# Narrow matmuls widened to 128 rows, a filter layer cast in three pieces, and a new table of issue, in a one-core transformer step

## The chip, the cores and the metric

The kernel runs on one NeuronCore of a Trainium2 chip. A core has a matrix engine (TensorE, PE in the rows below, with its weight loads shown apart as PEld), a vector engine (DVE), a scalar engine (ACT), a pool engine (POOL) and a queue that issues most of the transfers (SP). The metric is the time of one execution in microseconds on the device, the median of several executions.

## The reference

One inference step of a trunk with two layers runs over 128 prompt tokens and 1024 latent tokens, with 1024 channels in float32. Layer 0 mixes with a Hyena long convolution beside a latent attention (MLA); layer 1 with a Conformer convolution beside a grouped-query attention (GQA); each layer ends in an MLP of 4096 units. What the change touches is this (shapes cut, names as in the reference):

```python
# Hyena filters: 33 features -> 64 -> 64 hidden units -> 4 x 512 channels, for n_tok positions
hid = jnp.sin(freq * (z @ w1 + b1))
hid = jnp.sin(freq * (hid @ w2 + b2))
h = (hid @ w3) * jnp.exp(-t[:, None] * jnp.abs(decay))
spec = jnp.fft.rfft(two_sided(h), axis=0)
# long convolution, twice
z = gate * (irfft(rfft(z, 2 * n) * spec) + skip * z)
# MLP of every layer
f = jnp.square(jax.nn.relu(h @ w1 + b1)) @ w2 + b2
# grouped-query attention (prompt tokens attend to prompt tokens)
s = einsum('bqhgd,bkhd->bhgqk', q, k) * scale
```

## The kernel before

Every product with full precision is made from rounded parts: a matrix is held as a high part and a low part of a 32-bit format that TensorE takes in one pass, and `mm3` (L584) issues high x high, high x low and low x high into one PSUM bank. The helper lines are what the rows name: `mm` is L582, the transposes by the identity `tr` L590, `tt` (two tensors on DVE or POOL) L593, `ts` L597, `act` L603, `cpy` (copies and casts on ACT) L606, and `ld` (loads and stores on the SP queue) L562. All tiles lie in one arena, `b` in the rows, whose places come from a table.

The work is staged so: the Hyena filters are made (`filter_hidden`, then `ht` for eight tiles of 128 positions in two orders, then `spectra`), the input projections follow, then the long convolutions (`hyena`), MLA, the output projection, the MLP of layer 0 in three chunks of 384 tokens, and the same for layer 1. Beside the filters and the convolutions, matmuls with `ada_w` run (`ada_steps`, 32 output columns, not rounded).

Some matmuls contract over fewer than 128 rows of the array. In `filter_hidden` the features have 33 rows and the hidden units 64. In `ht` (L847) the 128-row part `hid` holds the high part in rows 0 to 63 and the low part in rows 64 to 127, and a second matmul with 64 rows adds high x low of `w3` (36 of them). In `hyena.first` (L1088) one extra matmul per 128 frequencies has 3 rows (`zrow` with `s3`, 16). In `mlp` (L1755) the bias `b2` enters through `ones` with 33 rows, of which rows 0 and 32 are filled (36). In GQA the prompt's second product has 64 rows (8).

The order in which each engine's instructions are issued is not that of the code. `in_order` (L2480) reads ORDER, a packed table with one step for each instruction of PE, DVE, ACT, POOL and SP, and ties every instruction to the one that the table puts ahead of it. Waits between engines follow from the data and from the reuse of places in the arena.

## Time and profile before

| | |
|---|---|
| three executions | 3310.30, 3310.32, 3315.06 us (median 3310.32) |
| the profiled execution | 3319.34 us |
| its span, first to last instruction | 3317.6 us |
| mean granted clock of TensorE | 0.983 of full |
| instructions | 40,881 |

The rows below come from the profiled execution. A row of instructions gives their start, busy time, engine, line, operation and operands (for a matmul rows\*columns of the weights, then rows x moving columns), their count, and in square brackets how long the engine was idle ahead of them and what ended that. PE's ends are modelled, so times from start to start are safer than busy times.

### The profile page before, as it was taken

To read this page: it belongs to the slowest core of one execution; us is meant where nothing else is said; L and a number is where in the kernel's file an instruction comes from. 1 tells how busy PE (TensorE), PEld (TensorE's weight loads), DVE (VectorE), ACT (ScalarE), POOL (GpSimd) and SP (SyncE) were. 2 spreads that over 40 slices of the span, in tenths; PEclk is the share of its full clock that TensorE was granted. 3 is DMA by queue.
4 is the path that set the end of the run, shared out by engine and by line. 5 is a ranking of instruction groups with operands and counts; after the bars stand their busy time and mean duration, and the time that the engine had idled before them with its cause. 6 is when DMAs were issued, how large, how long until landed. Compare 5 with 4: busy or idle time off the path is not lost. (4 is left out here: it accounts for less than half of the span.)

```text
span 3317.6 us, 40881 instructions
## 1 busy us (share of the span) xinstructions
PE 3185.1 (96%) x15636; PEld 2567.1 (77%) x15636; DVE 2106.3 (63%) x3088; ACT 1242.7 (37%) x2024; POOL 826.2 (25%) x713
## 2 busy tenths in 40 slices
...
PEclk9999888999999999999999998999999999999999
...
GB/s 224 185 42 148 254 142 132 96 19 43 106 118 219 150 143 210 170 155 174 100 156 156 125 167 119 46 48 46 126 116 188 156 133 162 139 100 181 137 127 102
DMA packets 161028, 444.58 MB, mean 134 GB/s; under 512 B 17384, under 2 KB 63144, under 8 KB 159296
## 3 DMA queue, kind: packets, MB, share of 16 engines
...
HBM read 386.10 MB, written 54.73 MB: 133 GB/s over the span
## 5 line engine op out<-in xcount | busy, mean ns | idle before, releaser
L582 PE MATMUL P<-b,b 128*128 128x384 f32 (+9 forms) x14314 | 2989.5, 375 | 91.3 <-ACT b L606 28.8
L582 PEld LDWEIGHTS P<-b,b 128*128 128x128 f32 (+3 forms) x14314 | 2443.3, 188 | 595.0 <-issue 150.1
L593 DVE TENSOR_TENSOR b<-b,b 128x1024 fp32r<-128x1024 f32 (+12 forms) x1087 | 952.6, 902 | 620.2 <-ACT b L606 383.0
L606 ACT CAST b<-b 128x1024 fp32r<-128x1024 f32 (+3 forms) x595 | 538.8, 918 | 1099.4 <-DMA b<-w 498.6
L593 POOL TENSOR_TENSOR b<-b,b 128x1024 f32<-128x1024 f32 (+10 forms) x440 | 670.2, 1540 | 924.6 <-ACT b L603 443.8
L603 ACT ACTIVATE b<-P 128x512 f32<-128x512 f32 (+4 forms) x400 | 221.6, 573 | 244.5 <-PE P L582 214.0
L597 POOL TENSOR_SCALAR small<-small 128x1 f32<-128x1 f32 (+2 forms) x72 | 41.8, 581 | 1049.8 <-DVE small L1682 1021.0
L593 DVE TENSOR_TENSOR b<-P,b 128x512 f32<-128x512 f32 (+11 forms) x364 | 214.3, 611 | 135.8 <-PE P L582 73.6
L1454 DVE TENSOR_REDUCE small<-P 128x1 f32<-128x512 f32 (+1 forms) x384 | 216.0, 591 | 45.1 <-PE P L582 41.6
L593 DVE TENSOR_TENSOR b<-b 128x384 f32<-128x384 f32 (+1 forms) x200 | 116.8, 597 | 199.0 <-ACT b L603 195.7
L600 DVE SCALAR_TENSOR_TENSOR b<-b,dwhalf,b 128x376 f32<-128x376 f32 (+2 forms) x268 | 204.2, 804 | 1.1
L603 ACT ACTIVATE b<-P,b 128x384 f32<-128x384 f32 x192 | 108.9, 577 | 220.0 <-PE P L582 212.5
L606 ACT COPY b<-P 128x512 f32<-128x512 f32 (+3 forms) x165 | 71.3, 449 | 199.9 <-PE P L582 157.6
L590 PE MATMUL P<-ident,b 128*128 128x128 f32 (+3 forms) x774 | 127.2, 287 | 18.2 <-DVE b L593 10.1
L590 PEld LDWEIGHTS P<-ident,b 128*128 128x128 f32 (+3 forms) x774 | 96.2, 146 | 55.7 <-DVE b L593 18.2
L603 ACT ACTIVATE b<-b 128x384 fp32r<-128x384 f32 (+2 forms) x200 | 102.3, 528 | 34.7 <-DVE b L593 16.6
L582 PE MATMUL P<-b,sT 128*32 128x512 f32 x384 | 100.0, 630 | 12.3 <-DMA b<-ada_w 12.2
L600 DVE SCALAR_TENSOR_TENSOR b<-b,small,b 128x1024 f32<-128x1024 f32 x72 | 93.0, 1295 | 7.0 <-POOL small L593 6.7
L606 ACT CAST b<-P 128x512 fp32r<-128x512 f32 (+9 forms) x134 | 64.3, 507 | 72.0 <-PE P L590 58.8
L603 ACT ACTIVATE b<-P,modT 128x384 fp32r<-128x384 f32 (+2 forms) x104 | 58.5, 596 | 75.6 <-PE P L582 37.6
L597 DVE TENSOR_SCALAR b<-P,modT 128x384 f32<-128x384 f32 (+2 forms) x104 | 58.5, 580 | 32.4 <-ACT b L603 25.6
L603 ACT ACTIVATE b<-b,dwhalf 128x429 f32<-128x429 f32 (+2 forms) x92 | 55.9, 626 | 56.8 <-PE P L582 27.7
...
## 6 DMA issues: line engine op xcount, KB each, us to landing
b<-w SPq DMA_DIRECT2D x384, 512.0 KB
...
```

The costliest lines, as they stand in the source:

```text
L582: self.nc.tensor.matmul(out, lhsT, rhs, start=start, stop=stop)
L590: self.nc.tensor.transpose(out, in_, self.ident)
L593: (eng or self.nc.vector).tensor_tensor(out=out, in0=a, in1=b, op=op)
L597: (eng or self.nc.vector).tensor_scalar(out=out, in0=a, scalar1=s1, scalar2=s2, op0=op0, **kw)
L600: self.nc.vector.scalar_tensor_tensor(out=out, in0=a, scalar=s, in1=b, op0=op0, op1=op1)
L603: self.nc.scalar.activation(out=out, in_=in_, func=func, **kw)
L606: self.nc.scalar.copy(out=out, in_=in_)
L1454: nc.vector.tensor_reduce(out=m3[i][:, 4 * jj + pi : 4 * jj + pi + 1], in_=b(w), axis=AX.X, op=ALU.max)
```

## The change

1. The 64-row matmul of `ht` gets 128 rows: `columns` now makes the low part of `w3` in all 128 rows.
2. The 3-row matmul of `hyena.first` gets 128 rows; `zrow` and each of the four `s3` tiles are set to zero on POOL first.
3. The 33-row bias matmul of `mlp` gets 128 rows, with zeros in the others.
4. The 64-row product of the GQA prompt gets 128 rows; `gqa_keys` makes the low part of the prompt's keys in all rows with one more DVE operation for each of two key heads.
5. `filter_hidden` casts and subtracts its last layer in three pieces of 384 columns instead of one of 1152.
6. The tables of issue are new for all five engines. The table of places is the same (its checksum alone changes, since it counts calls).

```diff
@@ filter_hidden
-        self.cpy(hid.r(n), dst.f(n))
-        self.tt(hid.r(n)[64:128], dst.f(n)[64:128], hid.r(n)[64:128], ALU.subtract)
+        for o in (0, 384, 768):
+            h, v = hid.r(384, o), dst.f(384, o)
+            self.cpy(h, v)
+            self.tt(h[64:128], v[64:128], h[64:128], ALU.subtract)
@@ filter_spectra, columns
-            self.tt(w3.r()[0:64], w3f.f()[0:64], w3h.r()[0:64], ALU.subtract)
+            self.tt(w3.r(), w3f.f(), w3h.r(), ALU.subtract)
@@ filter_spectra, ht
                 self.mm(b(), hs, w3h.r(512, cols), True, False)
-                self.mm(b(), hs[0:64], w3.r(512, cols)[0:64], False, True)
+                self.mm(b(), hs, w3.r(512, cols), False, True)
@@ hyena
         zrow = self.ra(512)
+        g.memset(zrow.f(512), 0.0)
...
             s3 = self.ra(256)
+            g.memset(s3.f(256), 0.0)
@@ hyena, first
-                            self.mm(out, zrow.r(128, 128 * q)[0:3], s3.r(256)[0:3], False, True)
+                            self.mm(out, zrow.r(128, 128 * q), s3.r(256), False, True)
@@ mlp
-        nc.vector.memset(b2.f()[0:33], 0.0)
+        nc.vector.memset(b2.f(), 0.0)
...
-        self.cpy(b2h[0:33], b2.f()[0:33])
+        self.cpy(b2h, b2.f())
...
-                            self.mm(banks[jj][s](), ones[0:33], b2h[0:33, 512 * s : 512 * s + 512], True, False)
+                            self.mm(banks[jj][s](), ones, b2h[:, 512 * s : 512 * s + 512], True, False)
@@ gqa_keys
-                self.tt(k2.r(n, o)[0:64], b(n)[0:64], k1.r(n, o)[0:64], ALU.subtract)
+                w = min(n, KEYS - o)
+                self.tt(k2.r(w, o)[0:64], b(w)[0:64], k1.r(w, o)[0:64], ALU.subtract)
+                if w < n:
+                    self.tt(k2.r(n - w, o + w), b(n - w, o=w), k1.r(n - w, o + w), ALU.subtract)
@@ gqa
-            return dict(m=full, row=lambda o, n: h.r(n, o), s=(full, h65), x=(full, h64), bufs=(a, h))
+            return dict(m=full, row=lambda o, n: h.r(n, o), s=(full, h65), x=(full, full), bufs=(a, h))
...
-            k64 = lambda o, n: k2.r(n, o)[0:64]
-            return dict(m=full, s=(full, k65), x=(full, k64))
+            low = lambda o, n: k2.r(n, o)
+            return dict(m=full, s=(full, k65), x=(full, low))
@@ the table of issue
-ORDER_OF = 1470002208
+ORDER_OF = 3602219959
```

The table is packed, so its effect is shown by what stands in three places. In these rows each line is an instruction with its output and inputs; buffer numbers are counted in the order of the code, and run four to nine higher in the new program.

**Place 1, the start, on ACT.** b_147 is the filters' last hidden layer, b_171 its rounded form, b_117 the decay rows, negt the positions. Before:

```order
L603 ACTIVATE b_121<-b_121 64x384 x3
L603 ACTIVATE b_147<-b_147 128x384 x3
L606 CAST b_171<-b_147 128x1152
L603 ACTIVATE b_147<-b_117 128x1024
L603 ACT_TABLE_LOAD
L603 ACTIVATE b_208<-b_147,negt 128x512
```

And now:

```order
L603 ACTIVATE b_121<-b_121 64x384 x3
L603 ACTIVATE b_147<-b_147 128x384
L606 CAST b_171<-b_147 128x384
L603 ACTIVATE b_147<-b_147 128x384
L606 CAST b_171<-b_147 128x384
L603 ACTIVATE b_147<-b_147 128x384
L606 CAST b_171<-b_147 128x384
L603 ACTIVATE b_147<-b_117 128x1024
L603 ACT_TABLE_LOAD
L603 ACTIVATE b_212<-b_147,negt 128x512
```

Each piece of the cast now follows its sine, so two of the three are done when the last sine is.

**Place 2, the MLP of layer 0, on PE.** The row with ones_r is a bias matmul; the other rows are matmuls of the running layers. Before:

```order
L582 MATMUL P<-b_10210,b_12280 128x384
L582 MATMUL P<-b_10277,b_12278 128x384 x2
L582 MATMUL P<-b_9191,ones_r 128x512
L582 MATMUL P<-b_12575,b_11811 128x512
L582 MATMUL P<-b_12577,b_11811 128x512
L582 MATMUL P<-b_12575,b_11811 128x512
L582 MATMUL P<-b_10277,b_12280 128x384
```

And now:

```order
L582 MATMUL P<-b_10286,b_12482 128x384
L582 MATMUL P<-b_10357,b_12480 128x384
L582 MATMUL P<-b_9200,ones_r 128x512
L582 MATMUL P<-b_12584,b_11820 128x512
L582 MATMUL P<-b_12586,b_11820 128x512
L582 MATMUL P<-b_12584,b_11820 128x512
L582 MATMUL P<-b_10357,b_12480 128x384
```

A bias matmul still stands alone between wide ones; what surrounds it is a later pair of columns (b_10357 for b_10277).

**Place 3, the last long convolution, on PE and SP.** b_4713 and b_4726 (and b_5267 before, b_5276 now) are transposed by ident; b_5267 and b_5276 hold the cached latents, loaded from c_ckv into the place that one of the transposed tiles of the convolution leaves. PE before:

```order
L582 MATMUL P<-b_3111,b_4597 128x256 x2
L582 MATMUL P<-b_3111,b_4599 128x256
L582 MATMUL P<-b_3113,b_4653 128x256 x2
L582 MATMUL P<-b_3113,b_4654 128x256
L582 MATMUL P<-b_3115,b_4668 128x256 x2
L582 MATMUL P<-b_3115,b_4669 128x256
L590 MATMUL P<-ident,b_5267 128x128 x2
L582 MATMUL P<-b_3109,b_4502 128x256 x2
```

PE now:

```order
L590 MATMUL P<-ident,b_4729 3x128
L582 MATMUL P<-b_4852,b_4754 128x512
L582 MATMUL P<-b_4851,b_4754 128x512
L590 MATMUL P<-ident,b_4713 128x128
L590 MATMUL P<-ident,b_4726 128x128
L590 MATMUL P<-ident,b_4713 128x128
L590 MATMUL P<-ident,b_4726 128x128
L590 MATMUL P<-ident,b_5276 128x128 x2
L582 MATMUL P<-b_4786,b_3104 128x256
```

And SP, before:

```order
L562 DMA b_5064<-spec_181 128x4x256
L562 DMA b_5141<-spec_181 128x4x256
L562 DMA b_5267<-c_ckv 128x256
L562 DMA b_5270<-c_kr 128x64
L562 DMA b_5228<-xd 128x1024
```

SP now:

```order
L562 DMA b_5073<-spec_185 128x4x256
L562 DMA b_5150<-spec_185 128x4x256
L562 DMA b_5237<-xd 128x1024
L562 DMA b_5276<-c_ckv 128x256
L562 DMA b_5279<-c_kr 128x64
```

The two transposes of the cached latents moved about 70 rows up on PE, right behind the last transposes of the convolution's input, while their load moved one place down on SP. The load waits for the last transpose of b_4713 in the new program, as it did for that of the same tile before, because it takes that tile's place.

## Rows read from the trace of the kernel before

**Rows 1.** The page of the profile: the span, the busy time of the engines, and the 40 slices of PE and of its granted clock:

```profile
span 3317.6 us, 40881 instructions
...
PE 3185.1 (96%) x15636; PEld 2567.1 (77%) x15636; DVE 2106.3 (63%) x3088; ACT 1242.7 (37%) x2024; POOL 826.2 (25%) x713
...
PEclk9999888999999999999999998999999999999999
```

**Rows 2.** The same by stages (start:end, length, busy time of each engine with the instructions that began, mean granted clock of TensorE, DMA share, GB/s). The first is the making of the filter tiles; the second row the long convolutions; the third goes through MLA and the MLP of layer 0 into the second mixer; the fourth the second half of the Conformer mixer and the start of GQA; the fifth the rest, with the MLP of layer 1; the last row is a part of the first:

```profile
0.00:120.00 120.00, 106.28 (x314) 52.69 (x315) 85.17 (x127) 59.62 (x94) 54.23 (x50) 1.00 0.51 187
...
340.00:605.00 265.00, 204.39 (x1194) 155.08 (x1193) 211.39 (x362) 63.08 (x128) 143.07 (x113) 0.88 0.54 177
605.00:2000.00 1395.00, 1381.60 (x6828) 1118.87 (x6827) 868.34 (x1279) 544.68 (x862) 306.78 (x263) 1.00 0.39 135
2000.00:2260.00 260.00, 234.17 (x1067) 155.86 (x1065) 235.31 (x363) 127.37 (x236) 178.20 (x138) 0.94 0.19 68
2260.00:3317.00 1057.00, 1041.90 (x5070) 877.04 (x5069) 602.24 (x826) 387.81 (x586) 113.56 (x79) 1.00 0.38 133
...
44.70:120.00 75.30, 75.30 (x270) 40.77 (x270) 62.64 (x85) 35.27 (x58) 39.52 (x28) 1.00 0.32 115
```

**Rows 3.** Who waited for whom, PE alone, in the stretch 340 to 605 us (engine, line, releaser: us in total, times, longest):

```profile
PE P L582 <- ACT b L606: 23.0, 11, 6.4
PE P L582 <- DMA b<-ada_w: 12.2, 4, 6.4
PE P L590 <- DVE b L593: 9.6, 4, 4.4
```

**Rows 4.** Matmul groups of the whole span, shapes kept apart (xcount | busy us, mean ns | idle before):

```profile
L582 PE MATMUL P<-b,b 64*128 64x512 f32 x36 | 21.9, 619 | 0.0
...
L582 PE MATMUL P<-b,ones_r 33*128 33x512 f32 x36 | 17.3, 490 | 1.1 <-ACT b L603 1.1
...
L582 PE MATMUL P<-b,b 3*128 3x256 f32 x16 | 6.1, 381 | 0.0
...
L582 PE MATMUL P<-b,b 64*128 64x128 f32 x8 | 2.6, 325 | 0.0
```

**Rows 5.** The timeline of PE: a run of wide matmuls, a run with four 64-row ones in it (its name is that of its first), and the row that follows each:

```profile
64.91 6.92 PE L582 MATMUL P<-b,b 128*128 128x512 f32 x29
71.76 2.76 PE L582 MATMUL P<-b,sT 128*32 128x512 f32 x10
74.45 4.65 PE L582 MATMUL P<-b,b 64*128 64x512 f32 x13
79.03 1.48 PE L582 MATMUL P<-b,sT 128*32 128x512 f32 x6
```

**Rows 6.** The timeline of the weight loads at the start of the second of these runs (64\*128 is the narrow one):

```profile
74.45 0.18 PEld L582 LDWEIGHTS P<-b,b 64*128 64x128 f32 x1 [0.84 <-issue]
74.88 0.19 PEld L582 LDWEIGHTS P<-b,b 128*128 128x128 f32 x1 [0.24 <-issue]
75.31 0.18 PEld L582 LDWEIGHTS P<-b,b 64*128 64x128 f32 x1 [0.25 <-issue]
```

**Rows 7.** The timeline of PE around two bias matmuls of the MLP of layer 0, with the run between them:

```profile
1392.76 0.49 PE L582 MATMUL P<-b,ones_r 33*128 33x512 f32 x1
1393.18 2.34 PE L582 MATMUL P<-b,b 128*128 128x512 f32 x9
1395.45 0.49 PE L582 MATMUL P<-b,ones_r 33*128 33x512 f32 x1
```

**Rows 8.** The timeline of ACT at the start: the cast of all 1152 columns behind the last sine, and the first ten exponentials:

```profile
19.76 1.15 ACT L606 CAST b<-b 128x1152 fp32r<-128x1152 f32 x1
...
24.70 6.23 ACT L603 ACTIVATE b<-b,negt 128x512 f32<-128x512 f32 x10
```

**Rows 9.** The timeline of DVE there: the subtraction for `hid`, and one of the multiplications of PSUM with an exponential:

```profile
20.94 1.35 DVE L593 TENSOR_TENSOR b<-b,b 64x1152 fp32r<-64x1152 f32 x1 [1.77 <-ACT b L606]
...
35.74 0.69 DVE L593 TENSOR_TENSOR b<-P,b 128x512 f32<-128x512 f32 x1 [2.17 <-PE P L582]
```

**Rows 10.** The timeline of PE there, the first row with all of 33 matmuls, and the row that follows:

```profile
22.35 22.46 PE L582 MATMUL P<-b,b 128*128 128x512 f32 x33 [4.89 <-DVE b L593]
44.74 3.16 PE L582 MATMUL P<-b,sT 128*32 128x512 f32 x8
```

**Rows 11.** The narrow matmuls among the 33 of that stretch, 22.3 to 44.7 us:

```profile
L582 PE MATMUL P<-b,b 64*128 64x512 f32 x16 | 12.0, 772 | 0.0
```

**Rows 12.** Busy time of PE's matmuls in two stretches that hold one shape alone, 128x256 (length, PE and PEld busy with their counts, granted clock, DMA share, GB/s):

```profile
2031.40:2037.30 5.90, 5.88 (x27) 5.88 (x28) 0.50 0.25 94
536.20:543.80 7.60, 7.60 (x63) 7.29 (x61) 1.00 0.63 194
```

**Rows 13.** The timeline of PE at place 3 of the change: two three-row transposes, and further on those of the cached latents:

```profile
525.20 0.38 PE L590 MATMUL P<-ident,b 128*3 128x128 f32 x2
...
543.80 0.38 PE L590 MATMUL P<-ident,b 128*128 128x128 f32 x2
```

**Rows 14.** The timeline of SP there: the issue of the loads:

```profile
524.18 0.57 SPq L562 DMA_DIRECT2D b<-c_ckv  x1
...
527.49 0.33 SPq L562 DMA_DIRECT2D b<-xd  x1
```

**Rows 15.** A load of 256 KB whose landing the profile gives (KB each, median us from issue to landing):

```profile
b<-pdft POOLq DMA_DIRECT2D x3, 256.0 KB, 3.3
```

More of the change, by code (lines that the diff above doesn't have):

```diff
@@ L64 @@
 HY_ENG = 0, 1, 0, 1
-PLACES_OF = 968071531
+PLACES_OF = 3472302832
 PLACES = """
@@ new lines @@
++iAL{*53#PXepfgz?+Zm?wHK2E1sxrj3j;m>aHcmF<eh|{nPbo~oT2~6aM<{cb0PA7nj;7CWj&h7XuX@`Jm<|0<O_1wYhP8y2oC=+o94MdXT2x8;qjQ
+~IKLBy=pQl(3y?BZ|B^wRvC31<!B`e^z9-K^Ia@Ui3p3C&?h?M&rl!J02bYszV)7VQ##d<W-
+0ejY)Lqt0q$ez5LR$kbHZPn1@$eOHW*R|QP3sTpVUiTdB6+Vd_xsMpW)mNu8aK){I23QMXFT79Q58lY9<hV`4W>Ujk>eK|-
++PJ>j;b<2x9{f5_A}0Fc=m6Xv`or2W=vg<z#})ZJX!l*m{a1Xu0~31QjQ0Lmwq_&t$pO_>mUNb!C67~>Rpy6)eY$QowXaNvzDMWjT6m<crLsQbjINEK
+S~9<7HiB-
+g=>mDBpKIqCS1HLg;Y;D#0kHYEkjaiVNA4vlZr0U*E413{`mFrF4Bt}Rs?=gdS3@eB<rFsW@pR4JqTH@OKUi_Z84>x9QNl&={CTG>YnjdG+uB>PUvnF
@@ new lines @@
+9xlP8bfyJLu6dVc#C|m1b-5G1>!<1;?_df0W{ZZf$w8TqaMK+zS7uzPP&!uN{afr<^t--*5|V1-
+$M6I4mjPwZ6_t<w<MyfFFD&d>)`zmhuiI0dfk`5ONdJnd9L1r1?f`mi2C@UAN(kp(V`v<QBKT@U>sQ;&x5W!=td+k7HD$WuU6Gg&dGHlXTcdi*4_1+X
+I0|1159xj+DEokJFAv|G-
+U{4OORLq?V+LuMfmO2FhpbdD3T649c~XJ?Mp}zyCU?pB&M$Q+ry4X5<>DwB)l!`N@x>bVokR_T+t)T6g%m3+K$?JkvMWhvY9dI=nka*0ALkPU_=PM;9
+T#F|DX9{jnOTI~)Er`w&aAlOHtFi~g}^-<#jDlR|deT2p-
+QPdPavy8Y1akzbSd%5Pv!yi@Tm#e!^wet4_AwZpR)ag`WW_4g)b#d>&+yejh!yhg5+H|YOuhP_f=3Cr+*RJ=;j?`nf!-
+lAs#F9kjuNd3czuRq!WkI=Pi9O4OG{QuGN$#5pz-
@@ new lines @@
+M2)By;TmQl#ymmP)7QM`xU+fDJy@D&RFC{*$IPU?uOUhMtMz-gp=WElA|Oq>J$I_tiJvX!>M5FCeI|wql^2+51Wp8Dm+TMF-
+rf$SZKq?Lw}@p^<lKB%j9F>Qu&+Ei}U5LLyp7pupaCk0iAm1EeWD7_0@1hcE&%3Gh<dp$3KNZNcB^b>POYPA2bqvRB=rh4QKTkmxswuCKzP-c-
+jzn`p|h<5g!}^zppSVV?MYvuc?#cJYWZ_&DY&$)`>xWq)v?XJQMN<nU!QP-WPVliII@bH_JUXKV3g9ekY7FM-L=Ep(WQ#7G1liA9YHPPjy%-
+X<K*#<et=qXtS8o)gbyb2>az+mqp@zI{jk1Ga64>fpXxD-
+e;5zW+e5Iac!TS#nh%6cW!;Pb5dP?&ZBBJ`&fnzotDquD|0?D9;VxNx+EtuKU8jyoz%X+u0!+fw#^#HC*NN7=-gB?XMXam3~uuSvc5E~PO3|-
+B=w;2%3lwBkG5-
+S7O5U|O_%N0dhqYv!r5yXE~va5$HF4scI^Orc9Vdj#XN^S`<dzZJ+R*N%B}|_$EOmm*x%1G81nD(RU8W6iw^tU<{u7=yTU8vg^FQikwH4nAVf>lBL~=
@@ new lines @@
+(h_Nu{MG9mPm{o;TZ(rIvoLljHT1MdqdVe70{|V&;!opz^0?mI`TPw69sjaNZZOwi5Gf%9-
+Sp=Frr$9DrhGZQ67SXp#6W#7&ze+In^~)AzTLk=Q9=RgvYzC<S^k*7UoUdBV2Z3Y^hCThqDGfX{SNEUUyKqT;=o|JH`o7uQWgpUkcreZzJ=i;IofQ_+
+gJ=`r3>4!2%lu2KHvRb(`+dwsALqBUZVwLPb<n#JG87&1E=rP+pOfmHP>Q7&z0d)7SX&-
+&@GN?aBl9YRWd;`7wCH}_=g)~XXQU#ga6gXQ$aum<Xz&oz5(g*>;U4iDc3IBUHl!^+l4Jy_0a>?4kuW#5^HDDv)#=c3uO@ab&j*!kx=Y+c9P1{(wGuj
+mKM`Q4UBDz9c1`8=0_nU?k>r}g)WXQ<SYY>Bh7{$@|)HvWM3MxfL(;nEIuFq10EcxH>pBS$zQmX}h6*3k}m<{Pt~rxPFaQT;pm`l@J8%zLPM&SEQAH8
+|#R-
@@ new lines @@
+LLRe#bcY2CGZ)&eYH_6E?!d41kxj0yQb8LczDk`c2!a|$^R#;uLIj%PKlw|$=*)?wNu+u3eIb?mdmPh-xh>VdlrL@i)eYG|i%`z^$Gm^FINt-GCl+3<
+eaCF${ehV;JADjkUDMCmW?i(+Haz!C2FQ*&Bm`6fl=ofPohI0osivUa2-
+<PqGVwb66L_OQt*pZ&K0oy4e_y(~KY5VE!EkY;PxpTj7K(Il&5ZEZJ>ItS_yFw^Uhs~Vt7#$T<S74Vh3V%nJdlZ)P-
+kR7*dw?))F;`J`qdta_I`DsdLo~qR5sX7LGRm<HkPl1*0#qwnNX?c?T6n=h0UL;SH7vkqKd4XIi&)1(ZRG@ggj{f82#_%}#art5STKHjkhWwB`U0$X?
+uaL{-
+<$8}npFbB~Dt{YZuD@R<AJ@+x)z5F%Gu|pMmA8m}{xd!LiSVc4CGscw>Eq!FdA+<ue_tgZ30KPh2(OdB(a$fGEA{v5q#{@8?<?g4;rCU)`%qYsXUekt
@@ new lines @@
+wNl4Z@}Y2#{9d?Q&X$w%SK%%_`W^XLIH6a+Q`>Nd{@gB~)bD&Ed_aHR8a^K05<V7g)?+v6IbYMhxl#4TH-
++ovjo~`^_3%}F`hU_VzgB;~B9D_V>(jqUKfg&ozfs;5-
+k>_*Z|JdKm#f0d!u#c=;pO4g`svr?ZF==z4OfJB%S*z$!@J}c!qwqd<cjdi`u96j)_%KO9o{BySMA`1;g{qE;TPos`2~4?c&j`wyhYB_UO6T|ubS<f<
+XQS;KY@(C7wffuIy_Tp{WHR=;F*85etvCub6_O?Yr<6_&vm#myx#Kw&z0Bdr~jnS^%iSIc#pR1z1nwgQT(QU=c@2QeE!|=C*cpU^ZMKL)7AR(j_?=Z?
+ctq@|Ec|CaV4MBZ+|-
+c=kQ+?za8Emek;5Wdx3lsmgheVf2UXYBq~jRS~XYO7vVE{jcdZ6hmR`07;aEK{BOfw>p5S9_G(ovK7+kBzM`Mfxa#XwFTO5(UEgn39r`-`?~U-
+HU8~=;PdDf%>hfRG|CZ&es`D1*TI>-Nt4qe+$Tpq-nuJQ}j9T!7QqzEMnAC7o*Ub@RuX4SHMBXVQ-
@@ new lines @@
+Xpiq}GY)#YB(%Gko?>Ur`=~F-
+F8{QM{TFvZbFAacgL;3XBnxhZn%Cd^JRjZqv6AeFx{%4=bEx=bI@)}uH<?Y(su0J0^WrWn6RtPVibW|r&to*%_CBZrQh-PEu#ACgZ=)(}6MURw+EnTj
+X+;UN!p@xXw(r+A8;?6%Hn6)hpU^6&L~gw#+<UK%<JMp1F)<sqooUu4>dDNCq(z&3UG(fp*1c^(1EAle0E#g!TrXT@dv%sXYP%OX=={8t>5a_5XPltr
+1a3lNp+3a@Gx<J-
+s^NTk?(ddcZ+auZ8m<fFxuaFTbBbLObsiDw6Rpg@v`eNCgWQI_+g|qDdSes1@)p`SslTU@ZCXQ>k1em(U=jXi6<@%Pd1J8i*fZD+<Ib9<n_HD3qsK;T
+mSB;h#lqTVyZACwnznwE;1*>bPc@h9HCsaEf`;?_7Nj1lvSFjcJwUljZUs+Qz@E>u*u`%iJvfGu+zzDNP4{ZqydBT#atN~gs~7`DW;apecP6tc@7H78
@@ new lines @@
+|Q+o8Ca9FCaE}a5T+d?%4s~cmMoPcZF{Iu8~MnP=of6YrpAK#2bfATb>8d`Wwm!E;wGY$))?FeX`+canUhH3p)XK=4<y45i1{?zdgBp%YUkn79;&N=_
+xbgSZ&utr<Wqf<)g{U+voq`x67Kt{7!Y!(a=`j@S;;<;k8W+|K9W-
+GBHs~9V5*FmAZ)HuXGud1^SieXP&!9G1!uZ*@kqcN+2)#}Qqfn}dg=~&$ZJHJ)9vTT~&kPDCF4!aWz$U^q{5au!amivovc9Nf^vt-
+(Rs%1PG=UKsZQ~GvIq7B-o?ZDWgV&=h2^_(cbH$%7P5%q?4=+->qi`GG|P0Q72xZY3QY#bbH0-
+6IO0#_g>+W)xYwM7hat<U=vX;0WM2YkFtzH5WWT7_0-
+1<lKbR}?hw$p%J`)#b|)IY$BKoF#3<>sx)idWbqAWAvt^5vak@%WRZrAM}VeW=<|Yl_agnORZwR6g@g4B%WN8jc4I)kMSn-
+&<5=5u@Ai0qCdMU{YGnT*(qPsBMdnP0%>gm(!e-
```

319 lines of the change are left out of this document (134 added, 185 removed).

## The prediction

> **What bounds the kernel now.** The page comes first: PE is busy for 96% of the span, the next engine, DVE, for 63% [rows 1]. So a term counts where PE's own time shrinks, or where PE waits. The stretches show where that is [rows 2]. From 605 to 2000 us PE is idle for 13.4 of 1395 us, from 2260 to the end for 15.1 of 1057: there PE's instructions are the time. From 340 to 605 it is idle for 60.6 of 265 us, DVE is busy for 211.4 and the mean granted clock is 0.88; from 2000 to 2260 it is idle for 25.8, DVE busy for 235.3, the clock 0.94. In these two stretches PE waits for others, in the first mostly for ACT's casts and for loads of `ada_w` [rows 3], and pays again by the lower clock. All idle time of PE is 132 us; the new table of issue can work on that, the wider matmuls on the rest.
>
> **What a narrow matmul costs.** Times from start to start tell it. A run of 29 matmuls with 128 rows and 512 columns goes from 64.91 to 71.76 us: 0.236 us each. The run of 13 with four 64-row ones takes 4.58 us, where 13 x 0.236 would be 3.07: 1.51 us more, 0.38 for each narrow one [rows 5]. The weight loads show how: narrow to wide 0.43 us, wide to narrow 0.43 us, so both neighbours of the switch are long, not the narrow matmul alone [rows 6]. Around a bias matmul with 33 rows, one narrow and nine wide ones take 2.69 us instead of 2.36: 0.33 more [rows 7]. I take 0.30 for each narrow matmul, a little under both because some narrow ones may follow each other and because nine wide ones between can hold small waits of their own; the bounds are 0.25 and 0.38. A widened matmul then costs what its wide neighbours cost, 0.236 us for 512 columns, and its number of columns is as before.
>
> On this the pages disagree. The Trainium skill, "TensorE: Matmul & The Clock Gate", section "Why this matters for your kernels", says that one matmul over few rows takes as long as one over 128; by that rule widening gives 0 us and only the table is left. The Trainium skill, "TensorEngine Tiling (Array Packing)", section "Key Properties", says that a change of tiling mode drains the engine. The trace agrees with the second: 0.43 us on both sides of a switch against 0.236 without one.
>
> **The terms.**
> - Bias, 36 matmuls [rows 4], 18 in each of the two stretches where PE is nearly never idle. Place 2 of the change shows that they stay alone between wide ones, so without the change each would still pay. 34 to 36 x 0.30: 10.4 us (9 to 13.7). All of it is on the path.
> - Filter tiles, 36 matmuls [rows 4], 16 of them before 44.7 us [rows 11]. The 20 later ones lie in a stretch where PE has no gap (it is busy for all of the 75.3 us from 44.7 to 120 [rows 2]): 20 x 0.30 = 6.0 us (5 to 7.6).
> - The start, 22.35 to 44.74 us: 33 matmuls in 22.39 us, 0.68 each [rows 10], so the alternation that takes 0.43 later takes 0.68 here. That is TensorE's lower level (1.2 GHz), though the column of the clock says nothing low there. No wide run at that level with 512 columns is in the trace; one of 256 columns takes 0.22 at a granted clock of 0.50 against 0.12 at 1.00, 1.8 times [rows 12], so I estimate 0.236 x 1.8 = 0.42 and 33 x 0.42 = 14.0 us, 8.4 less. Ahead of it, the cast of 1152 columns starts at 19.76 and the subtraction ends at 22.29 [rows 8, 9]; with place 1 only the last third stands behind the last sine, about 0.4 + 0.5 us: 1.6 us earlier. Together 10.0. But then others are next: the exponentials start at 24.70 and take 0.62 each [rows 8], the multiplications that free the banks 0.69 [rows 9]; seventeen of these end at about 37.0, so PE can't hand on much before 37.5: 7 us. I take 7, with 10.0 above and 0 below, if the tiles are split and added no earlier than now.
> - Long convolutions, 16 three-row matmuls [rows 4] x 0.30 = 4.8 us, in the stretch where DVE is busy for 80% and PE waits. I count half, 2.4 (0 to 4.8).
> - GQA's prompt, 8 matmuls of 128 columns [rows 4]: no wide run of that form is in the trace. The bounds are 0 and 8 x 0.30 = 2.4; I take 1.5, since they lie in the last part of the kernel with little idle time on PE.
> - What is added: two DVE subtractions in `gqa_keys`, two more casts and two more subtractions in `filter_hidden`, five memsets on POOL, which is busy for 25% of the span [rows 1]. The pieces are shorter and hide behind the sines; if the cover is gone, some 0.1 us of fixed cost for each, under 1 us in all. 0.
> - Place 3: before, the load of the cached latents is issued at 524.18, 19.6 us ahead of its transposes at 543.80 [rows 13, 14]. Now the transposes stand right behind the last transposes of the tile whose place the load takes, so the load can't be issued until PE is there, and on SP it stands behind the load of `xd`, which was issued at 527.49. Everything behind it on PE waits. A 256 KB load lands 3.3 us after its issue [rows 15], this one has 128 KB: a loss of 3 us, bounds 0 (if PE would wait there for DVE anyway) and 6 (with the clock that a gap costs in this stretch).
> - The rest of the table moves most instructions of PE by some tens of places and those of SP by two or so. Nothing in the trace says whether that is good. I count 0, with 20 us to either side: a quarter of the 86 us that PE is idle in the two stretches where it waits.
>
> Sum: 10.4 + 6.0 + 7 + 2.4 + 1.5 - 3 = 24.3 us. The profiled execution took 3319.3 (its span 3317.6 and 1.7 around it), 9.0 more than the median of 3310.3. So 3295 for such an execution, and 3286 for the median.
>
> **The rivals.**
> 1. The table finds much more. For: 132 us of idle PE, 60.6 in one stretch, where loads of `ada_w` alone held it for 12.2 us, and a clock that comes back when gaps close. Against: DVE is busy there for 80%, and place 3 shows a tighter, not a looser, load. A third of the 86 us, with 10 us by the clock, on top of the 24: some 3250.
> 2. The time that PE saves turns into waiting, in the filter tiles too: only bias and prompt stay, 11.9 - 3 = 9 us, or less with a worse table. For: DVE is busy for 62.6 of the 75.3 us after 44.7 [rows 2]. Against: PE has no gap there. Some 3301 to 3312.
> 3. Slower, by the SP queue in the long convolutions. SP issues in order and each load may wait for a place; where PE's next work stands right behind such a load, as in place 3, each microsecond that SP holds it is one of PE's, and a gap of some microseconds brings the lower clock, which at 0.88 over 265 us may already cost that stretch up to 32 (0.12 x 265). Ten such places at 3 us each would be needed before the gain of 27 is gone; the order shows one that is clear. 3318 to 3330.
> 4. Widening gives nothing: a narrow matmul waits for something that a wide one in its place waits for too, such as the banks. For: nothing but that the rows don't name what the 0.43 us are. Against: they come with each switch, in the tiles and in the MLP alike [rows 6, 7]. Then 3310 + 3 = 3313. The first of the two pages of the Trainium skill, "TensorE: Matmul & The Clock Gate", would end here.
>
> **How the numbers follow.** The forecast (3272 to 3301) gets 0.62, rival 1 0.19, rival 2 0.10, rival 3 0.07, rival 4 0.02. A difference under 0.2%, 6.6 us, can't be told from none here: three executions already lie 4.8 us apart. Faster is the forecast, rival 1 and the 0.04 of rival 2 that lie under 3303.7: 0.85. Within it lie the other 0.06 of rival 2, rival 4 and 0.01 of rival 3: 0.09. Slower is the rest of rival 3: 0.06. The range 3252 to 3306 takes in most of rival 1 and the better half of rival 2 and leaves 2 in 10 out.
>
> **What would show it.** In the changed trace no matmul group with 3, 33 or (but for the first six) 64 rows is left; a bias matmul starts 0.23 to 0.25 us ahead of its follower; the first 33 tile matmuls end by 38 us instead of 44.7, at 0.42 us or less each. The stretches of the two MLPs are shorter by 5 us each. PE waits for a DMA of `c_ckv` of about 3 us near 520. The forecast is wrong if start to start stays at 0.43 beside a widened matmul, if PE's idle time in the convolutions grows by over 15 us, or if it falls by over 20.

## The result, and the profile after

The changed kernel takes 3272.79 us, the median of four executions (3269.45 to 3274.99), beside 3311.01 us for the kernel before (four executions, 3310.30 to 3315.06). The ratio is 0.9881, with a 95% interval from 0.9864 to 0.9898: 38 us less. The forecast was 3286 us, 24 less, with 3252 to 3306 as its range. Three executions of the kernels told of below, two of `old_in_conv` and one of `latents_later`, took 6192 to 7095 us and are left out of every median.

The profiled execution took 3274.27 us, its span 3272.5. That is 45.1 us under the profiled span of before [rows 1], but the profiled execution of before was a long one, 9.0 over its median, so the two traces show some 7 us more than the medians do. The page after: span, busy time of the engines, and the granted clock in 40 slices.

```profile
span 3272.5 us, 40881 instructions
...
PE 3150.7 (96%) x15636; PEld 2566.2 (78%) x15636; DVE 2127.9 (65%) x3092; ACT 1244.3 (38%) x2026; POOL 830.9 (25%) x718
...
PEclk9999988999999999999999998999999999999999
```

Three stretches, with the same columns as in [rows 2]; the last is the part of the filter tiles in which PE has work throughout:

```profile
340.00:605.00 265.00, 213.41 (x1263) 167.03 (x1264) 230.64 (x387) 73.24 (x140) 148.63 (x142) 0.88 0.52 170
...
2000.00:2260.00 260.00, 245.06 (x1107) 151.84 (x1106) 242.25 (x376) 130.55 (x244) 162.81 (x108) 0.97 0.16 55
...
44.70:105.30 60.60, 60.15 (x252) 37.70 (x251) 51.80 (x72) 34.44 (x55) 35.06 (x23) 1.00 0.42 146
```

In the convolutions PE is idle for 51.6 of 265 us (60.6 before), from 2000 to 2260 for 14.9 (25.8 before, though the work there is that of 35 us later now), and the clock is 0.88 as it was and 0.97 instead of 0.94. In the filter tiles it is idle for 0.5 of 60.6 us; they end some 14 us earlier.

Over the span, PE's busy time fell by 34.4 us [rows 1] and its idle time by about 10.7 (the rest of the 45.1). So most of the gain lies in what PE's own instructions take, as the forecast had it, and some in shorter waits.

Stretches at fixed times hold different work in the two kernels, so I compare in another way below. PE's matmuls are counted by their moving columns, which are the same number in every kernel here, and the table says how far another kernel is behind the changed one when it has passed the same number of columns. The profile of each kernel gives one row (the kernels are told of with their experiments). How far two executions of the same work differ is seen where a kernel's work is still that of the changed one: by up to 1.6 us ahead of 330 us (`old_in_two_places`, at 62), 2.8 by 605 (`bias_65_rows`) and 4.4 by 1000 (`narrow_bias`, whose first bias matmul comes only at 1063). Differences below that are not told from none.

```
behind the changed kernel, us, at equal columns of PE
at us of changed    62    105    330    605    840   1000   1800   2400   3200
before             8.2   14.6   14.9   27.1   27.6   21.8   34.9   31.5   45.2
narrow_again       3.2    8.2    8.8   11.3   11.4   11.8   18.4   20.7   26.5
old_table          2.0    4.9    5.1   14.0   16.3   10.6   18.0   11.0   17.9
narrow_bias        0.0   -0.2   -0.8   -2.2   -2.0   -4.4    3.2    2.0    8.8
narrow_tiles       3.7    8.7    8.6    9.1    9.3    9.4   10.1    5.8    5.8
old_in_conv        0.0   -0.2   -0.5    8.2    8.8    8.1    8.6   10.9   10.8
changed_again      0.5    0.0   -0.2   -1.4   -1.3   -1.0    0.6   -2.5   -2.9
```

PE's waits in the stretch 340 to 605 us (releaser: us in total, times, longest), to be read beside [rows 3]: ACT's casts 14.8 instead of 23.0, `ada_w` 9.0 instead of 12.2, and the wait for `c_ckv` that place 3 announced, 3.0 us:

```profile
PE P L582 <- ACT b L606: 14.8, 6, 7.4
PE P L590 <- DVE b L593: 9.6, 6, 3.1
PE P L582 <- DMA b<-ada_w: 9.0, 2, 5.0
...
PE P L590 <- DMA b<-c_ckv: 3.0, 1, 3.0
```

And around two bias matmuls of the MLP of layer 0, to be read beside [rows 7]: the bias matmul (128 rows) starts 0.22 to 0.24 us ahead of its follower, as any wide one does, where it was 0.42.

```profile
1360.07 0.39 PE L582 MATMUL P<-b,ones_r 128*128 128x512 f32 x1
1360.29 1.55 PE L582 MATMUL P<-b,b 128*128 128x512 f32 x6
1361.68 0.40 PE L582 MATMUL P<-b,ones_r 128*128 128x512 f32 x1
1361.92 5.48 PE L582 MATMUL P<-b,b 128*128 128x512 f32 x23
1367.24 0.40 PE L582 MATMUL P<-b,ones_r 128*128 128x512 f32 x1
```

### The profile page after: what moved, and what is told of

It reads as the page before. It is cut to its first block, busy times and chain, and to the rows that moved or that the text cites. A ratio compares the mean times of both kernels' runs of the same rounds, so it can differ in the third digit from the quotient of the medians.

```text
span 3272.5 us, 40881 instructions
## 1 busy us (share of the span) xinstructions
PE 3150.7 (96%) x15636; PEld 2566.2 (78%) x15636; DVE 2127.9 (65%) x3092; ACT 1244.3 (38%) x2026; POOL 830.9 (25%) x718
## 4 chain that ended last, share of the span: by engine, by line
PE 83%; DVE 9%; DMA 2%; issue 2%; POOL 2%; ACT 2%; SPq 0%; POOLq 0%; DVEq 0%; ACTq 0%
PE P L582 81%; DVE b L593 5%; PE P L590 2%; DVE b L600 2%; DVE small L1458 1%; POOL b L593 1%; ACT b L606 1%; ACT b L603 1%; DMA b<-w 1%; DMA b<-yd 0%; DMA uu<-b 0%; DMA b<-ada_w 0%; DVE b L597 0%; DVE b L1518 0%; POOL small L593 0%
## 5 line engine op out<-in xcount | busy, mean ns | idle before, releaser
L582 PE MATMUL P<-b,b 128*128 128x384 f32 (+6 forms) x14314 | 2968.6, 374 | 79.2 <-ACT b L606 20.4
L593 DVE TENSOR_TENSOR b<-b,b 128x1024 fp32r<-128x1024 f32 (+12 forms) x1089 | 969.4, 913 | 641.9 <-ACT b L606 466.8
L606 ACT CAST b<-b 128x1024 fp32r<-128x1024 f32 (+4 forms) x597 | 539.3, 916 | 1080.5 <-DMA b<-w 498.7
L600 DVE SCALAR_TENSOR_TENSOR b<-b,dwhalf,b 128x377 f32<-128x377 f32 (+2 forms) x268 | 211.2, 824 | 0.9
L590 PE MATMUL P<-ident,b 128*128 128x128 f32 (+4 forms) x774 | 127.3, 286 | 22.1 <-DVE b L593 11.2
L590 PEld LDWEIGHTS P<-ident,b 128*128 128x128 f32 (+4 forms) x774 | 94.0, 145 | 64.7 <-issue 13.2
L603 ACT ACTIVATE b<-b 128x384 fp32r<-128x384 f32 (+2 forms) x200 | 103.0, 529 | 25.2 <-DVE b L593 14.8
L582 PE MATMUL P<-b,sT 128*32 128x512 f32 x384 | 91.5, 623 | 9.0 <-DMA b<-ada_w 9.0
```

The source lines that it names most:

```text
L582: self.nc.tensor.matmul(out, lhsT, rhs, start=start, stop=stop)
L590: self.nc.tensor.transpose(out, in_, self.ident)
L593: (eng or self.nc.vector).tensor_tensor(out=out, in0=a, in1=b, op=op)
L600: self.nc.vector.scalar_tensor_tensor(out=out, in0=a, scalar=s, in1=b, op0=op0, op1=op1)
L603: self.nc.scalar.activation(out=out, in_=in_, func=func, **kw)
L606: self.nc.scalar.copy(out=out, in_=in_)
```

## The experiments

Theory A is the prediction's: a narrow matmul costs about 0.3 us beside its neighbours, and that time is on the path. Rival B says that the table of issue is the gain; C that PE's saving turns into waiting except at the bias. D, E, F, G and H belong to single experiments. Each kernel is the changed one with one thing altered, timed beside the kernel before on the same chip.

### All narrow matmuls back, new table kept

```diff
-self.mm(b(), hs, w3.r(512, cols), False, True)
+self.mm(b(), hs[0:64], w3.r(512, cols)[0:64], False, True)
-self.mm(out, zrow.r(128, 128 * q), s3.r(256), False, True)
+self.mm(out, zrow.r(128, 128 * q)[0:3], s3.r(256)[0:3], False, True)
-self.mm(banks[jj][s](), ones, b2h[:, 512 * s : 512 * s + 512], True, False)
+self.mm(banks[jj][s](), ones[0:33], b2h[0:33, 512 * s : 512 * s + 512], True, False)
...
-low = lambda o, n: k2.r(n, o)
+low = lambda o, n: k2.r(n, o)[0:64]
```

> The changed kernel, its new table of issue kept, with all 96 narrow matmuls back at their 3, 33 and 64 rows (the zeroed tiles, the split cast and the added subtractions stay). Theory A (each narrow matmul costs about 0.30 us beside its neighbours, on the path, as in the sum of the prediction): about 26 us come back, 3296 to 3302 us. Rival B (the gain is the table's, the widening gives little): 3270 to 3278 us. Rival C (the saving of PE turns into waiting outside the MLPs, so only the bias counts): 3282 to 3286 us.

Measured: 3298.05 us (3294.3 to 3300.8), ratio to before 0.9962 (0.9950 to 0.9975). That is 25.3 us above the changed kernel. Rivals B and C fall. The two traces have the same order, so the prices can be read instruction by instruction, from the start of the matmul ahead to the start of the narrow or widened one, and from there to the start of the next, summed over all of a kind:

```
                      into + out of it, us in total     medians, narrow    medians, 128 rows
                      narrow   128 rows   difference     into    out        into    out
tiles (36)             37.7      25.4       12.2         0.431   0.430      0.245   0.236
bias (36)              26.4      16.2       10.3         0.319   0.424      0.226   0.232
3-row (16)              8.7       4.8        4.0         0.210   0.310      0.119   0.118
prompt (8)              3.6       2.0        1.6         0.152   0.254      0.062   0.131
```

The sum is 28.1 us of PE's time (128 rows from a second profile of the changed kernel), of which the clock on the wall shows 25.3. For the bias and the 3-row matmuls the price is the same by the medians, 0.09 us on the way into a narrow matmul and 0.19 on the way out, 0.28 each, with 512 columns as with 256. The prompt's, with 128 columns, pay 0.09 and 0.12. The tiles cost more: 16 of them stand in the slow start, and some later ones alternate with single wide ones, 0.43 us on both sides.

### The table of before, with the widened matmuls

```diff
-for x, step in enumerate(steps of the new table):
+for x, step in enumerate(steps of the table before, the 11 added instructions put in):
```

> The changed code (all widened matmuls, the cast in pieces) with the table of issue of the kernel before; the 11 added instructions stand right behind their siblings or where the new table has them, the three pieces of the cast together where the one cast stood. Theory A: the widening keeps its 24 to 26 us and the table's share is lost, 3284 to 3288 us. Rival B: 3308 to 3313 us, nearly all is the table's. Rival C: 3298 to 3302 us, the bias alone.

Measured: 3292.13 us (3286.5 to 3297.4), ratio 0.9945 (0.9931 to 0.9958): 17.3 us under before, 19.3 above the changed kernel. Between A and C. With the experiment above: the table (with the cast in pieces) alone gives 11.4 us (3309.5 to 3298.1), on top of the widening 19.3; the widening gives 17.3 with the old table and 25.3 with the new. Each of these differences is known to some 6 us, so whether the two edits really help each other by 8 us is left open. What is clear is that the table is not the 0 of the sum.

### The bias alone, at 33 and at 65 rows

```diff
-self.mm(banks[jj][s](), ones, b2h[:, 512 * s : 512 * s + 512], True, False)
+self.mm(banks[jj][s](), ones[0:33], b2h[0:33, 512 * s : 512 * s + 512], True, False)
```

> The changed kernel with only the 36 bias matmuls back at 33 rows. Theory A: 10.4 us (9 to 13.7) slower than the changed kernel, 3282 to 3286 us, 5 us in each MLP; in the trace 0.43 us from start to start on both sides of a bias matmul. Rival B: within 3 us of the changed kernel.

Measured: 3285.81 us (3283.1 to 3292.9), ratio 0.9931 (0.9918 to 0.9943): 13.0 us above the changed kernel, as theory A said; rival B falls. By the profiles it is 8.8, but this execution was 4.4 us ahead at 1000 us, where no bias matmul has run yet; from 1000 to 2000 it loses 7.7 us and from 2400 to the end 6.8. The weight loads around two bias matmuls (one row for each run of equal ones):

```profile
1359.18 0.18 PEld L582 LDWEIGHTS P<-b,ones_r 33*128 33x128 f32 x1 [0.36 <-issue]
1359.60 1.22 PEld L582 LDWEIGHTS P<-b,b 128*128 128x128 f32 x6 [0.24 <-issue]
1361.19 0.18 PEld L582 LDWEIGHTS P<-b,ones_r 33*128 33x128 f32 x1 [0.37 <-issue]
1361.62 4.46 PEld L582 LDWEIGHTS P<-b,b 128*128 128x128 f32 x20 [0.25 <-issue]
```

From 1359.18 to 1359.60 is 0.42 us, from 1361.19 to 1361.62 0.43: the way out. The same with 65 rows:

```diff
-self.mm(banks[jj][s](), ones, b2h[:, 512 * s : 512 * s + 512], True, False)
+self.mm(banks[jj][s](), ones[0:65], b2h[0:65, 512 * s : 512 * s + 512], True, False)
```

> The changed kernel with the 36 bias matmuls at 65 rows instead of 128. Theory A (the price hangs on the switch between a matmul of up to 64 rows and one of more, not on the number of rows): as the changed kernel, 3270 to 3276 us, and 0.23 to 0.24 us from start to start on both sides. Rival D (each change of the number of rows costs, or a matmul of half the rows costs in proportion): 3279 to 3286 us, as with 33 rows (3285.8).

Measured: 3273.4 us (3269.1 to 3276.2), ratio 0.9883 (0.9870 to 0.9895), the changed kernel's own. From start to start it is 0.230 us into a bias matmul behind one of 512 columns and 0.234 out of it. Theory A holds, rival D falls: it isn't the difference in rows that costs: 65 rows beside 128 are free, 64 or 33 are not.

### The filter tiles alone, and in pairs

```diff
-self.mm(b(), hs, w3.r(512, cols), False, True)
+self.mm(b(), hs[0:64], w3.r(512, cols)[0:64], False, True)
```

> The changed kernel with only the 36 matmuls of the filter tiles back at 64 rows. Theory A: the 33 matmuls of the start take 0.68 us each again and the 20 later ones 0.30 more, 11 to 13 us slower than the changed kernel, 3284 to 3286 us, all of it before 120 us. Rival C: since DVE's multiplications and ACT's exponentials bound the tiles, 0 to 4 us slower, 3273 to 3277 us.

Measured: 3278.67 us (3276.4 to 3283.3), ratio 0.9907 (0.9894 to 0.9921): 5.9 us slower than the changed kernel, half of what theory A said and more than C. By the table above it is 3.7 us behind at 62 us and 8.7 at 105: the start gives 3.7 instead of 7, the 20 later tiles 5.0 instead of 6.0. Of the 8.7 us some 3 are gone by 2400 us, within what two executions differ by there. PE at the start, in this kernel, then in old_table, then in the changed one (first row: all matmuls of one shape without a gap):

```profile
17.91 27.19 PE L582 MATMUL P<-b,b 128*128 128x512 f32 x42 [1.07 <-DVE b L593]
45.03 1.68 PE L582 MATMUL P<-b,sT 128*32 128x512 f32 x4
```

```profile
20.72 5.22 PE L582 MATMUL P<-b,b 128*128 128x512 f32 x13 [3.31 <-DVE b L593]
26.10 1.33 PE L582 MATMUL P<-b,b 128*128 128x512 f32 x4 [0.16 <-DVE b L593]
27.97 0.96 PE L582 MATMUL P<-b,b 128*128 128x512 f32 x3 [0.54 <-DVE b L593]
29.19 4.35 PE L582 MATMUL P<-b,b 128*128 128x512 f32 x13 [0.27 <-DVE b L593]
33.47 1.91 PE L582 MATMUL P<-b,sT 128*32 128x512 f32 x8
```

```profile
17.89 6.24 PE L582 MATMUL P<-b,b 128*128 128x512 f32 x16 [1.06 <-DVE b L593]
25.70 1.96 PE L582 MATMUL P<-b,b 128*128 128x512 f32 x6 [1.58 <-DVE b L593]
```

Narrow, 42 matmuls take 27.1 us, 0.65 each, PE without a gap: PE is the bound. Wide, 13 take 5.2 and 16 take 6.2, 0.39 to 0.40 each, and now there are gaps that DVE ends (1.58 us ahead of 25.70): the multiplications are the next bound, as the prediction feared. Later ACT holds PE too (2.18 us ahead of 37.33), and from 33 to 43 us the granted clock is 0.50. So about half of the start is eaten.

The mean of 0.39 hides two speeds. In the changed kernel the wide matmuls start 0.427 us apart up to 22.75 us, then 0.235. From 37.9 to 39.2 us, where the granted clock is 0.50, they are again 0.427 apart, so the first 5 us ran at the lower level (1.2 GHz), though the clock's column says 1.00 there. In the kernel with narrow ones, alternating narrow and wide ones start 0.72 us apart up to 43 us, where the same alternation later takes 0.43: by these times PE stayed at the lower level all along. What widening gave at the start is thus also an earlier rise of the clock.

In the next kernel the 64-row matmuls of two tiles stand together. Fifteen such pairs were meant, and the expectation counts on them; the trace has 12, so 48 switches and not 42, and only four of the pairs lie behind 62 us, not six (PE's order):

```
 b_180,b_171 128x512 x2    two tiles' first products, 128 rows
 b_181,b_171 128x512 x2    their second products, 64 rows
 b_180,b_171 128x512 x2
 b_181,b_171 128x512 x2
```

> As narrow_tiles (the tile matmuls at 64 rows again, table of the changed kernel), but in 15 pairs of tiles the two 64-row matmuls stand next to each other, so the switches between 64 and 128 rows are 42 instead of 70; no matmul is added or taken away. Theory A (the price is 0.19 us at each switch): the six pairs behind 60 us give 2.3 us back, those of the start 1 to 2, so 5 to 6.5 us behind the changed kernel at 150 us, where narrow_tiles was 8.7 behind; 0.23 to 0.24 us from the first of a pair to the second. Rival D (a narrow matmul costs by itself, wherever it stands): 8.7 behind at 150 us, and 0.43 from the first to the second.

Measured: 3283.67 us (3275.0 to 3286.8), ratio 0.9909 (0.9893 to 0.9925), not to be told from narrow_tiles. It is 8.6 us behind at 150 us, where narrow_tiles is 8.7, which is rival D's number; but it is 4.8 instead of 3.7 behind at 62 us, and from there to 105 us it loses 3.9 more instead of 5.0. Both differences are within what two executions differ by, so the matmuls themselves have to tell. The weight loads of one late pair and of its follower:

```profile
65.69 0.29 PEld L582 LDWEIGHTS P<-b,b 64*128 64x128 f32 x2 [0.37 <-issue]
66.34 1.69 PEld L582 LDWEIGHTS P<-b,b 128*128 128x128 f32 x8 [0.35 <-issue]
```

Two narrow ones take 0.65 us from the first to the wide one behind them. By the starts of the matmuls of this pair it is 0.33 us on the way in, 0.33 from the first to the second, and 0.32 on the way out, which is 0.42 behind a lone one: 0.98 us, where three wide ones take 0.71. So this pair costs 0.27 us; the other three late ones cost 0.28, 0.27 and 0.31. That is what a lone narrow one costs (0.28). From the first to the second neither theory was right (0.236 by A, 0.43 by D), but rival D's principle falls: the price is paid once for a run of narrow matmuls, however the 0.28 us lie among the starts, and not once for each. Runs of one and of two were measured; four pairs save 4 x 0.28 = 1.1 us. At a fixed price of 0.19 for each switch, A's, they would have saved 1.5.

### The cast in one piece

```diff
-for o in (0, 384, 768):
-    h, v = hid.r(384, o), dst.f(384, o)
-    self.cpy(h, v)
-    self.tt(h[64:128], v[64:128], h[64:128], ALU.subtract)
+self.cpy(hid.r(n), dst.f(n))
+self.tt(hid.r(n)[64:128], dst.f(n)[64:128], hid.r(n)[64:128], ALU.subtract)
```

> The changed kernel with the last layer of the filters cast and subtracted in one piece again, where its last piece stood in the new order. Theory A, by the term of the sum: the first tile matmul starts at some 22 us instead of 17.9, but ACT's exponentials and DVE's multiplications are the bound behind it, so 1 to 2 us slower by 105 us, 3273 to 3276 us. Rival H (the pieces are what the start gained): 4 us or more slower by 105 us, 3276 to 3279 us.

Measured: 3272.8 us (3266.2 to 3277.8), ratio 0.9877 (0.9859 to 0.9895). Rival H falls: the first tile matmul starts at 22.82 us instead of 17.89, 26 of them then run without a gap, and the kernel is 1.5 us behind at 105 us and 0.8 at 330. That is theory A's number, but two executions of one kernel differ by as much there, so it isn't told from 0.

```profile
22.82 8.19 PE L582 MATMUL P<-b,b 128*128 128x512 f32 x26 [5.18 <-DVE b L593]
31.47 0.96 PE L582 MATMUL P<-b,b 128*128 128x512 f32 x3 [0.46 <-DVE b L593]
```

### The order of before in the long convolutions

All five engines keep the new order, but the instructions that the changed kernel issues from 335 to 620 us are put among themselves into the order of before.

> The changed kernel; the instructions that it issues between 335 and 620 us stand among themselves in the order of the kernel before, on all five engines. Theory E (about half of what the new table gives lies in the long convolutions: at equal work of PE the old table lost 5 us up to 335 and 14 up to 620): 9 us slower than the changed kernel, 3280 to 3284 us, with PE's waits for casts of ACT back at some 20 us there. Rival F (what the table gains there is taken back at the next place where others bound): 3271 to 3277 us.

Measured: 3280.9, 3285.1, 3290.0 and 3292.7 us, median 3287.5, ratio 0.9925 (0.9912 to 0.9939), 14.8 us above the changed kernel and more than E said; by the profile 8.2 us behind at 605 us and 10.8 at the end. Theory E holds, F falls: the convolutions are where the table gives most. PE's waits there:

```profile
PE P L582 <- ACT b L606: 23.1, 9, 6.8
PE P L590 <- DVE b L593: 9.0, 4, 4.4
PE P L582 <- DVE b L593: 8.5, 5, 4.0
PE P L582 <- DMA b<-ada_w: 7.3, 2, 4.7
```

The casts of ACT hold PE for 23.1 us again, as before (23.0), instead of 14.8. That goes with the gain; no run changes these casts alone, so that they are its cause is likely, not shown.

### The cached latents

```diff
 L590 MATMUL P<-ident,b_4726 128x128
-L590 MATMUL P<-ident,b_5276 128x128 x2
 L582 MATMUL P<-b_4786,b_3104 128x256
...
 L582 MATMUL P<-b_4786,b_3104 128x256
+L590 MATMUL P<-ident,b_5276 128x128 x2
```

> The changed kernel with the two transposes of the cached latents 12 matmuls further down on PE (place 3), all else kept. Theory A, as in the sum: the load of c_ckv holds PE for 3.0 us there, the matmuls behind it go ahead meanwhile, 1.5 to 3 us faster by 605 us. Rival G (PE would wait there for DVE anyway, whose sums for the next convolution end at 507 to 508 us): within 1 us by 605 us; in the time both lie within 3270 to 3276 us.

Measured: 3267.6, 3270.8 and 3271.5 us, ratio 0.9877 (0.9860 to 0.9894). PE at place 3, in the changed kernel, then with the transposes later (in square brackets the idle time ahead, and what ended it):

```profile
504.89 0.66 PE L590 MATMUL P<-ident,b 128*128 128x128 f32 x4 [0.35 <-DVE b L593]
508.56 0.69 PE L590 MATMUL P<-ident,b 128*128 128x128 f32 x2 [3.01 <-DMA b<-c_ckv]
508.90 5.89 PE L582 MATMUL P<-b,b 128*128 128x256 f32 x24
514.62 0.60 PE L590 MATMUL P<-ident,b 128*128 128x128 f32 x4
```

```profile
504.49 0.66 PE L590 MATMUL P<-ident,b 128*128 128x128 f32 x4 [0.38 <-DVE b L593]
507.35 2.04 PE L582 MATMUL P<-b,b 128*128 128x256 f32 x12 [2.20 <-DVE b L593]
509.22 0.38 PE L590 MATMUL P<-ident,b 128*128 128x128 f32 x2
510.55 1.69 PE L582 MATMUL P<-b,b 128*128 128x258 f32 x12 [0.95 <-ACT b L606]
```

The first shows the prediction's 3 us word for word: 3.01 us for the load of `c_ckv`. In the second that wait is gone, and PE waits 2.20 us for DVE at the same place and 0.95 for ACT a little later: 3.15. That is rival G's picture: the wait was forecast right, and without it PE waits for others. The position at 605 us, by which the two theories were to be told apart, doesn't settle the price: this profile is 3.2 us ahead of the changed kernel's there, as A said, but four executions with the changed kernel's work up to there are 1.4 to 2.8 ahead too. From 504 to 530 us this kernel gains 2.1 us, and the second kernel of the next section, with the same edit, 0.4; kernels without it gain 0 to 1.7 there. So the price is hardly more than 2 us, may be 0, and the time doesn't show it.

### One place where the old order was better

From 840 to 1000 us the old table catches up by 5.7 us (16.3 to 10.6 in the table of columns). All engines, one after the other, in the changed kernel:

```profile
835.46 12.68 POOL L593 TENSOR_TENSOR b<-b,b 128x1024 f32<-128x1024 f32 x5
...
841.58 8.11 DVE L593 TENSOR_TENSOR b<-b,b 128x384 fp32r<-128x384 f32 x2 [0.24 <-PE P L582]
...
849.61 0.28 DVE L1560 COPY b<-P 128x128 f32<-128x128 f32 x1
...
849.94 0.45 PE L590 MATMUL P<-ident,b 128*96 128x128 f32 x1 [2.47 <-DVE b L1560]
```

The row at 841.58 holds two operations of DVE and is named for its first. That one, 128x384, takes 6.98 us where one of its kind takes 0.55 (last section); the other, 128x1024, takes 1.2 as usual. POOL runs five of its own from 835.46 to 848.14, and DVE is free soon after they end. DVE's copy and PE's transpose stand behind it, PE waits 2.47 us, and from then on the granted clock is 0.51 for 10 us:

```profile
848.60:858.80 10.20, 8.86 (x24) 5.40 (x26) 2.38 (x7) 2.32 (x6) 2.37 (x1) 0.51 0.25 88
859.00:2000.00 1141.00, 1122.77 (x5657) 965.49 (x5654) 713.49 (x987) 417.87 (x621) 210.46 (x211) 0.99 0.47 157
```

So in this execution 2.5 us of waiting cost 5 to 6. That is not the rule. Nine other profiles with this order here have the same gap, 2.5 to 2.9 us: in six of them the granted clock over the same 10.2 us is 0.50 to 0.67, in two 0.83, and in one, `one_cast_2`, 1.00:

```profile
848.70:858.90 10.20, 8.93 (x42) 4.50 (x44) 5.24 (x11) 2.98 (x8) 2.37 (x1) 1.00 0.27 98
```

That kernel gets 4.2 us ahead of the changed one between 840 and 860 us, and `narrow_bias` (0.83) 2.6. What decides whether the clock falls is left open. Two kernels have the order of before at this place, the first also from 2095 to 2300 us, the second also the latents later.

> The changed kernel; the instructions issued between 825 and 880 us and between 2095 and 2300 us stand among themselves in the order of the kernel before, on all engines. There the old table lost less at equal work of PE: 5 us less at the first place, where PE waits 2.5 us for DVE and then runs at a granted clock of 0.50, and 4 to 5 less at the second. Theory E (the table's effect is a sum over places that hardly touch each other): 8 to 10 us faster than the changed kernel, 3262 to 3266 us. Rival F (a gain at one place is waited away at the next): 3270 to 3275 us.

> The changed kernel with two edits of the order alone: the instructions issued between 825 and 880 us in the order of the kernel before, and the transposes of the cached latents 12 matmuls later. Theory E (the profile gave 4.7 us at the first place and 2 to 3 at the second, and places add up): 5 to 8 us faster than the changed kernel on the same chip, 3265 to 3268 us. Rival F (waited away later, or within what differs from one execution to the next): 3270 to 3275 us.

Measured: the first 3271.05 us (3268.8 to 3275.6), ratio 0.9878 (0.9866 to 0.9891); the second 3268.78 (3267.2 to 3270.2), ratio 0.9867 (0.9850 to 0.9883), beside the changed kernel on the same chip:

> The changed kernel itself, as the yardstick on the chip of the three runs beside it. All theories: 3269 to 3276 us, as in the result.

It took 3272.28 us (3267.4 to 3277.9), ratio 0.9879. In both traces the place gives some 6 us between 840 and 1000 us, beside a trace of the changed kernel in which the clock fell. Here is the second kernel: DVE is still slow beside POOL (5.5 us), but the transposes of PE no longer stand behind it:

```profile
845.00 8.39 POOL L593 TENSOR_TENSOR b<-b,b 128x1024 f32<-128x1024 f32 x3 [0.98 <-ACT b L603]
...
845.68 5.46 DVE L593 TENSOR_TENSOR b<-b,b 128x384 fp32r<-128x384 f32 x2 [1.16 <-PE P L582]
...
851.53 0.29 DVE L1560 COPY b<-P 128x128 f32<-128x128 f32 x1 [0.39 <-PE P L582]
...
852.85 0.27 PE L590 MATMUL P<-ident,b 128*96 128x128 f32 x1
```

The other place, 2095 to 2300, gives nothing (5.4 us ahead at 2000, 5.6 at 2400): there two executions of one kernel differ by 3 us, and what I read from one pair of profiles was that. In the time the second kernel is 3.5 us faster than the changed one, which its interval does not tell from no change. The first lies where rival F has it (3270 to 3275), not at theory E's 3262 to 3266; the second between the two. So the medians don't show the 6 us of the traces, though their intervals don't exclude them. That the gap does not bring the low clock every time may be a part of it.

## Why the prediction was right, and where it was off

- **The mechanism** was right: a narrow matmul between wide ones makes its neighbourhood long, and 128 rows take that away. Rival 4 said that widening gives nothing; it gave 17 to 25 us, and 25.3 with the new table, beside the 27.3 of the sum without place 3 (1.6 of it for the cast). A lone narrow one costs 0.28, where 0.30 was taken. Behind a wide matmul of 512 columns a bias matmul takes 0.327 us in and 0.423 out with 33 rows, 0.230 and 0.234 with 65. The rule of the Trainium skill behind rival 4, "TensorE: Matmul & The Clock Gate", section "Why this matters for your kernels" (a single matmul over 32 rows takes as long as one over 128), does not carry over to one between wide ones here. The rule of the Trainium skill, "TensorEngine Tiling (Array Packing)", section "Key Properties" (a change of tiling mode drains the engine), fits a price that is paid once for a run of narrow ones (0.27 to 0.31 us for a pair, 0.28 for a lone one).
- **Bias**, 10.4: 10.3 from start to start; 13.0 between medians, 8.8 between profiles that differ by 4.4 ahead of the first bias matmul.
- **Later tiles**, 6.0: 5.0. **Start**, 7: 3.7 with the new table, where others bound sooner than thought and the sixteenth tile's second matmul starts at 39.20 us (44.02 before), later than the sign of 38 us for the end; with the old table 6.2 (8.2 less 2.0 at 62 us), and the 33 tile matmuls end at 33.5 us instead of 44.7. The 0.42 us at the lower level came out (0.427), but after 5 us the wide ones leave that level, which the sum did not have; that 7 was near with the old table is in part luck. The cast in pieces, 1.6: 1.5 by 105 us, 0.8 after, not told from 0.
- **3-row matmuls**, half of 4.8: 4.0 from start to start; 2.2 by 605 us (11.3 less 9.1), which is half but no more than two executions differ by there. **Prompt**, 1.5: 1.6 from start to start.
- **Place 3**, -3: 0 to -2. The wait came, 3.0 us at 508.6. The weak step is "Everything behind it on PE waits": so it did, but without that wait PE waits 3.15 us for DVE and ACT. The other bound, 0, had been named.
- **The rest of the table**, 0 +- 20: 11 to 19. This is the term that was mis-sized ("Nothing in the trace says whether that is good. I count 0"), and it makes most of the 13 us between forecast and median. That the range held rests on the 20 us put to either side of it. By the row of `old_table` the gain lies in the convolutions (9 us), the first 100 us (5), and at two places in the MLPs, near 1740 and 2875 us of the changed kernel, where the old table has PE wait 2.0 and 2.7 us for ACT and the granted clock is then 0.62 to 0.66 for some 5 us (4 to 5 us each). Between 840 and 1000 us, and perhaps from 2000 to 2400, the new table takes back some. Rival 1 had the place right and the size too large.
- **The signs.** PE's idle time in the convolutions fell by 9 us, under the 20 named, and a bias matmul starts 0.22 to 0.24 us ahead of its follower. The six 33-row matmuls of `filter_hidden` are still there; the sign had left them out.
